# A two-layer hybrid encoder on one core: the butterflies and products of its Hyena branch on one elementwise engine instead of two

## The chip, the core and the metric

The kernel runs on one core of a Trainium2 chip. A core has a matrix engine (TensorE, PE in the profile), an elementwise engine (VectorE, DVE), an engine for functions of one operand (ScalarE, ACT), a third elementwise engine (GpSimd, POOL), and a queue from which most DMAs are issued (SyncE, SP). TensorE writes its results to PSUM; all other working data lie in SBUF. Each engine works through its own queue of instructions in order and waits on semaphores for the others.

The metric is the device time of one execution in microseconds (us), the median of several runs.

## The reference

The reference is an encoder trunk of two layers on 512 tokens of width 1024, all in float32:

```python
for i in range(DEPTH):                                   # DEPTH = 2
    hn = rmsnorm(h, ln_mix[i])
    (aq, ak, av, hy, gq, gk, gv, go, glr, gates) = split_cols(hn @ w_in[i], IN_SPLITS)
    y_a = attention_mixer(aq, ak, av, ...) @ w_br_attn[i]
    spec = hyena_filter_spectra(z_pos, window, hy_w1[i], ...)        # long filters, as spectra
    y_b = hyena_mixer(hy, hy_conv[i], spec, hy_skip[i]) @ w_br_hyena[i]
    y_c = gla_mixer(gq, gk, gv, go, glr, ...) @ w_br_gla[i]
    gate = jax.nn.sigmoid(gates.reshape(B, L, N_BRANCH, D_MODEL))
    mixed = gate[:, :, 0] * y_a + gate[:, :, 1] * y_b + gate[:, :, 2] * y_c
    h = h + mixed @ w_out[i]
    h = h + memory_cross_attention(rmsnorm(h, ln_x[i]), rmsnorm(mem, ln_mem[i]), ...)
    h = h + jnp.square(jax.nn.relu(rmsnorm(h, ln_mlp[i]) @ mlp_w1[i])) @ mlp_w2[i]

def long_conv(u, spec, skip):                            # u is (1, 512, 512 channels)
    y = jnp.fft.irfft(jnp.fft.rfft(uf, n=2 * L, axis=1) * spec, n=2 * L, axis=1)[:, :L]
    return (y + uf * skip).astype(u.dtype)

def hyena_mixer(u, conv_w, spec, skip):
    u = short_conv(u, conv_w)                            # width 3, on v, x1 and x2
    v, x1, x2 = jnp.split(u, 3, axis=-1)
    z = x1 * long_conv(v, spec[:, 0], skip[0])
    return x2 * long_conv(z, spec[:, 1], skip[1])
```

What matters here is the Hyena branch: for each layer two long convolutions in a row, each a forward transform, a product with a filter's spectrum, and an inverse transform.

## The kernel before

All large products are done by three matmuls in a 32-bit format that TensorE rounds (`mm3`, L249): an operand is split into a rounded high half and the rest, and high x high, high x low and low x high are added in PSUM (L251, L252, L253). The high half is made by ScalarE (L235), the low one by VectorE as a subtraction (L236). Weights arrive in chunks of 128x1024 (`wr`), and every chunk is split in the same way into `wh` and `wl`, with three buffers each. So every product, and the split of every weight chunk, has a step on VectorE.

**The Fourier transforms are matmuls.** A transform of 1024 points is taken apart into four small ones of 128x128 cosine and sine matrices (`dft`) and butterflies between their results. A spectral product (`spectral`, L798) is done for 256 channels and one of the two convolutions of a layer. There are thus four for a layer: `hyena_half` runs for c = 0 and 1, and each half runs the two convolutions one after the other (o = 0 and 1), since the second works on the result of the first. One spectral product does the following:

- it loads four tiles F of the filter's spectrum (128x512 each) from device memory;
- forward matmuls into PSUM, four tiles; ScalarE copies two of them to SBUF (`held`), VectorE adds and subtracts the other two to and from these (L611, `ts`);
- the butterfly `quarters` (L614): four results from the sums; two by one wide instruction each (128x512, L618 and L619), two by two narrow ones each (128x256, L622);
- the complex products with F, for each of the four results g: two wide multiplications (L823, L824) and two narrow additions (L825, L826);
- the inverse butterflies: L830 to L834, then four wide L838, each followed by a split of its result into `pqh` (ScalarE) and `pql` (VectorE);
- inverse matmuls with `dft` into PSUM.

After the first convolution the result is multiplied by x1 into `z` (L870), which is split for the next one. After the second it is copied by ScalarE to `yt`, transposed by TensorE, and scaled and multiplied by x2 on VectorE into `yb` (L887).

**The filters** (`filters`, L637) are computed for each layer, for both convolutions and both halves: a small network on position features, a window, matmuls with `dft`, and at the end the same `quarters` (L749) into four tiles `ff`, which go to device memory as F (L751). Layer 0's run ahead of the attention, between about 100 and 290 us. Layer 1's run as pieces within layer 0's MLP.

**Which engine does what** is told for these parts by a table of letters, V for VectorE and P for GpSimd (L170). `engs` (L221) turns a row of it into engines. `fq` and `hq` are the four results of `quarters` in the filters and in a spectral product; `hp` the four complex products; `hi` the inverse butterflies, the first four letters L830 to L834, the last four the four L838:

```python
ENGS = dict(fq='PPVV', hq='VVPV', hp='VVPV', hi='VVVVPVPV', lx='VVVVVVVV', aw='V',
            mx='VPVPVPVP')
```

GpSimd also has other work that the table doesn't tell: the adds of the merge (L1117, three branches into `acc`), sums of the filters (L673, L674, L711).

**What sets the order.** The branches are generators; ORDER0 and ORDER (L145 to L156) list the order in which their steps are written out (`hy0`, `hy1` are the two halves of Hyena, `me` the merges, `ga` the gates). On that a scheduler puts each engine's queue in order, by what is ready when by its own cost model, with priorities: splits of weights are put ahead by 200 (SPLIT_AHEAD), late steps back by the numbers of LATE (L167), as the inverse matmuls (`hc`, 100). While Hyena's steps run, TensorE also has the projections of gates and branches to do (`xh`, `xl` with `wh`, `wl`; `yah`, `ych`), which need only weights.

Of the kernel before, what the change touches and what calls it, by code (L numbers as in the profile page):

```python
# [93 lines left out]
def laid_out(a):  # L94
# [43 lines left out]
    for s_ in range(2):  # L138
# [28 lines left out]
LATE = dict(ff=50, fn=100, fr=100, fs=50, gA=100, gm=35, go=150, gq=35, gs=150, gt=10, hc=100, ht=150,  # L167
            kt=300, pt=100, pv=150, qt=200, xs=200, xt=35, xv=10)

ENGS = dict(fq='PPVV', hq='VVPV', hp='VVPV', hi='VVVVPVPV', lx='VVVVVVVV', aw='V',  # L170
            mx='VPVPVPVP')
SMALL = 768

# [1 line left out]
class Trunk:  # L175
# [45 lines left out]
    def engs(self, key):  # L221

        return [self.nc.vector if x == "V" else self.nc.gpsimd for x in ENGS[key]]

# [1233 lines left out]
```

## Time and profile before

| | |
|---|---|
| median of 3 runs | 2281.23 us (2280.59 to 2283.82) |
| profiled execution, its own time | 2285.21 us |
| its span | 2283.4 us |
| mean granted TensorE clock | 0.985 of full speed |
| TensorE busy | 2197.6 us, 96%, 11032 matmuls |
| VectorE busy | 1533.5 us, 67%, 2455 instructions |
| ScalarE busy | 1001.0 us, 44%, 1623 instructions |
| GpSimd busy | 422.6 us, 19%, 353 instructions |
| DMA | 233.56 MB, mean 102 GB/s |

Busy times are shares of the span. In the rows of this document L236 is line 236 of the kernel; a row of a group gives the line, the engine, the operation, the tile written, the tiles read, their shape (partitions x elements) and type, the count, the busy time in us, the mean duration of one in ns, and the idle time of the engine just before them with the engine, tile and line that ended most of it.

Hyena's products run from about 410 to 600 us (layer 0) and from about 1530 to 1720 us (layer 1). VectorE's busy share is highest in the first 300 us (0.9 and more in some slices), where layer 0's filters and attention lie.

### The profile page before, as it was taken

To read this page: it belongs to the slowest core of one execution; us is meant where nothing else is said; L and a number is where in the kernel's file an instruction comes from. 1 tells how busy PE (TensorE), PEld (TensorE's weight loads), DVE (VectorE), ACT (ScalarE), POOL (GpSimd) and SP (SyncE) were. 2 spreads that over 40 slices of the span, in tenths; PEclk is the share of its full clock that TensorE was granted. 3 is DMA by queue.
4 is the path that set the end of the run, shared out by engine and by line. 5 is a ranking of instruction groups with operands and counts; after the bars stand their busy time and mean duration, and the time that the engine had idled before them with its cause. 6 is when DMAs were issued, how large, how long until landed. Compare 5 with 4: busy or idle time off the path is not lost.

```text
span 2283.4 us, 28957 instructions
## 1 busy us (share of the span) xinstructions
PE 2197.6 (96%) x11032; PEld 1831.6 (80%) x11032; DVE 1533.5 (67%) x2455; ACT 1001.0 (44%) x1623; POOL 422.6 (19%) x353
## 2 busy tenths in 40 slices
PE   7989999998899999999999989999989999999999
PEld 5877888786678878888887878887867888888887
DVE  7798855979665765766485685667886566344445
ACT  6666844332344544443335576343323444433231
POOL 1142101224220101111060230102252101000004
PEclk9999999999999999999999999999989999999999
DMA  6442123223143243433344211332232322333332
GB/s 236 136 139 83 56 84 116 65 83 106 59 148 112 63 127 102 134 120 100 100 155 146 94 51 56 91 117 74 77 109 91 130 75 74 102 99 95 98 94 95
DMA packets 80098, 233.56 MB, mean 102 GB/s; under 512 B 9174, under 2 KB 11222, under 8 KB 79960
## 3 DMA queue, kind: packets, MB, share of 16 engines
q1 hardware_dynamic: 76792, 225.95, 31.2%
q0 software_dynamic: 3168, 5.77, 0.9%
q8 instruction: 86, 1.41, 0.3%
q14 instruction: 52, 0.43, 0.1%
HBM read 214.91 MB, written 16.78 MB: 101 GB/s over the span
## 4 chain that ended last, share of the span: by engine, by line
PE 78%; DVE 14%; issue 3%; ACT 2%; DMA 2%; POOL 1%; SPq 0%; DVEq 0%; POOLq 0%; ACTq 0%
PE ps L251 24%; PE ps L253 24%; PE ps L252 24%; DVE wl L236 3%; PE ps L557 1%; DVE ts L823 1%; ACT wh L235 1%; PE ps L566 1%; DMA F<-F 1%; PE ps L568 1%; DVE u L824 1%; PE ps L544 1%; DVE ts L611 1%; PE ps L545 0%; DMA wr<-in_w_in_dram 0%
## 5 line engine op out<-in xcount | busy, mean ns | idle before, releaser
L236 DVE TENSOR_TENSOR wl<-wr,wh 128x1024 fp32r<-128x1024 f32 x324 | 415.1, 1284 | 244.0 <-ACT wh L235 239.7
L235 ACT CAST wh<-wr 128x1024 fp32r<-128x1024 f32 (+1 forms) x328 | 341.0, 1042 | 507.1 <-PE ps L252 424.2
L253 PE MATMUL ps<-xh,wl 128*128 128x512 f32 x1344 | 530.6, 395 | 17.5 <-DVE wl L236 17.5
L251 PE MATMUL ps<-xh,wh 128*128 128x512 f32 x1344 | 532.9, 397 | 4.2 <-ACT wh L235 3.9
L252 PE MATMUL ps<-xl,wh 128*128 128x512 f32 x1344 | 531.1, 395 | 0.0
L253 PEld LDWEIGHTS ps<-xh,wl 128*128 128x128 f32 x1344 | 254.6, 189 | 73.8 <-DVE wl L236 22.5
L251 PEld LDWEIGHTS ps<-xh,wh 128*128 128x128 f32 x1344 | 254.8, 190 | 58.2 <-ACT wh L235 5.5
L252 PEld LDWEIGHTS ps<-xl,wh 128*128 128x128 f32 x1344 | 254.9, 190 | 50.0
L253 PE MATMUL ps<-hdh,wl 128*128 128x512 f32 x512 | 199.4, 390 | 0.0
L252 PE MATMUL ps<-hdl,wh 128*128 128x512 f32 x512 | 199.4, 390 | 0.0
L251 PE MATMUL ps<-hdh,wh 128*128 128x512 f32 x512 | 199.2, 389 | 0.0
L1374 DVE TENSOR_TENSOR macc<-ps,macc 128x512 f32<-128x512 f32 x96 | 65.9, 690 | 89.1 <-PE ps L253 88.9
L252 PEld LDWEIGHTS ps<-hdl,wh 128*128 128x128 f32 x512 | 96.1, 188 | 19.9
L253 PEld LDWEIGHTS ps<-hdh,wl 128*128 128x128 f32 x512 | 96.1, 188 | 19.8
L251 PEld LDWEIGHTS ps<-hdh,wh 128*128 128x128 f32 x512 | 96.1, 188 | 19.7
L1376 POOL TENSOR_TENSOR macc<-macc,rb 128x512 f32<-128x512 f32 x16 | 23.5, 1469 | 398.4 <-DVE macc L1374 398.4
L251 PE MATMUL ps<-wh,xh 128*128 128x256 f32 x320 | 91.7, 286 | 0.0
L252 PE MATMUL ps<-wl,xh 128*128 128x256 f32 x320 | 91.5, 286 | 0.0
L253 PE MATMUL ps<-wh,xl 128*128 128x256 f32 x320 | 91.1, 285 | 0.0
L1358 DVE TENSOR_TENSOR rl<-rl 128x512 f32<-128x512 f32 x64 | 44.6, 697 | 64.8 <-ACT rl L1357 64.8
L352 POOL TENSOR_TENSOR hsum<-hsum,hsq 128x512 f32<-128x512 f32 x30 | 43.6, 1454 | 168.3 <-ACT hsq L350 168.3
L1357 ACT ACTIVATE rl<-ps 128x512 f32<-128x512 f32 x64 | 37.9, 592 | 77.9 <-PE ps L253 77.9
(405 smaller groups left out, 4522.1 us busy)
## 6 DMA issues: line engine op xcount, KB each, us to landing
wr<-in_mlp_w_dram SPq DMA_DIRECT2D x128, 512.0 KB, 3.6
wr<-in_w_in_dram SPq DMA_DIRECT2D x108, 512.0 KB, 3.7
wraw<-in_x_wv_dram SPq DMA_DIRECT2D x16, 512.0 KB, 5.5
wr<-in_x_wk_dram SPq DMA_DIRECT2D x16, 512.0 KB, 3.7
F<-ff SPq DMA_DIRECT2D x32, 256.0 KB, 3.2
F<-F SPq DMA_DIRECT2D x32, 256.0 KB, 4.9
wr<-in_w_out_dram SPq DMA_DIRECT2D x16, 512.0 KB, 3.6
wr<-in_x_wq_dram SPq DMA_DIRECT2D x16, 512.0 KB, 3.7
```

Of the source, the lines that this page charges most:

```text
L235: r = self.nc.scalar.copy(hi, src)
L236: (lo_eng or self.nc.vector).tensor_tensor(lo, src, hi, op=ALU.subtract)
L251: mm(out, lh, rh, start=start, stop=False, skip_group_check=True)
L252: mm(out, lh, rl, start=False, stop=False, skip_group_check=True)
L253: mm(out, ll, rh, start=False, stop=stop, skip_group_check=True)
L352: eng.tensor_tensor(self.hsum, self.hsum, sq, op=ALU.add)
L544: nc.tensor.matmul(s, QH[:, tk], K2, start=True, stop=False)
L557: nc.tensor.transpose(pt[:, k, i * P:(i + 1) * P], Pn[i][:, (2 * kp + k) * P:(2 * kp + k + 1) * P], self.ident)
L1357: nc.scalar.activation(r, ps, AF.Relu)
L1358: nc.vector.tensor_tensor(r, r, r, op=ALU.mult)
L1374: nc.vector.tensor_tensor(acc[m], ps, acc[m], op=ALU.add)
L1376: nc.gpsimd.tensor_tensor(acc[m], acc[m], rb, op=ALU.mult)
```

## The change

Four entries of the table of engines are rewritten, so that no letter P is left in them:

```diff
-ENGS = dict(fq='PPVV', hq='VVPV', hp='VVPV', hi='VVVVPVPV', lx='VVVVVVVV', aw='V',
+ENGS = dict(fq='VVVV', hq='VVVV', hp='VVVV', hi='VVVVVVVV', lx='VVVVVVVV', aw='V',
             mx='VPVPVPVP')
```

With it these instructions go from GpSimd's queue to VectorE's: in each of the eight spectral products the two narrow halves of one result of L622, one each of L823, L824, L825 and L826, and two of the four L838; in each of the eight filters L618 and L619. `mx` and the adds that are written with `nc.gpsimd` stay as they are. The operations, tiles and buffers are the same; the scheduler orders all queues anew.

In VectorE's queue in layer 0's filters this is the difference (a - stands before the change, a + after it). `ts` are the sums of L611, `held` what ScalarE copied, `ff` the filter's results, `wl` the low half of a weight chunk, made of `wr` and `wh`:

```order
 L611 TENSOR_TENSOR ts_868<-ps_825,held_852 128x512
-L236 TENSOR_TENSOR wl_75<-wr_69,wh_71 128x1024
+L618 TENSOR_TENSOR ff_870<-ts_866,ts_802 128x512
+L619 TENSOR_TENSOR ff_871<-ts_866,ts_802 128x512
 L622 TENSOR_TENSOR ff_872<-ts_868,ts_806 128x256 x2
 L622 TENSOR_TENSOR ff_873<-ts_868,ts_806 128x256 x2
+L236 TENSOR_TENSOR wl_75<-wr_69,wh_71 128x1024
```

L618 and L619 are in VectorE's queue now, and the weight's low half comes after the four `ff` instead of ahead of them.

In layer 0's first spectral product VectorE's queue read like this before, from the last multiplications to the first `pql`. `u` and `held` are the four results that are multiplied by F, L781 and L783 the short convolution of another step, L1113 a merge:

```order
L825 TENSOR_TENSOR u_4351<-u_4351 128x256
L831 TENSOR_TENSOR ts_4346<-held_4324,u_4350 128x512
L781 SCALAR_TENSOR_TENSOR u_4269<-ps_4244,consts,u_4269 128x511
L826 TENSOR_TENSOR u_4351<-ts_4348 128x256
L783 SCALAR_TENSOR_TENSOR u_4269<-ps_4244,consts,u_4269 128x511
L832 TENSOR_TENSOR ts_4328<-held_4344,u_4351 128x512
L833 TENSOR_TENSOR ts_4348<-held_4344,u_4351 128x256
L834 TENSOR_TENSOR ts_4348<-u_4351,held_4344 128x256
L236 TENSOR_TENSOR wl_75<-wr_70,wh_71 128x1024
L236 TENSOR_TENSOR pql_4551<-held_4324,pqh_4550 128x512
```

After the change the same place reads:

```order
L825 TENSOR_TENSOR held_4344<-held_4344 128x256
L781 SCALAR_TENSOR_TENSOR u_4269<-ps_4244,consts,u_4269 128x511
L826 TENSOR_TENSOR held_4344<-ts_4328 128x256
L783 SCALAR_TENSOR_TENSOR u_4269<-ps_4244,consts,u_4269 128x511
L825 TENSOR_TENSOR u_4351<-u_4351 128x256
L1113 SCALAR_TENSOR_TENSOR acc_4390<-gt_1720,ps_4377 128x512
L826 TENSOR_TENSOR u_4351<-ts_4348 128x256
L236 TENSOR_TENSOR wl_75<-wr_70,wh_71 128x1024
L830 TENSOR_TENSOR ts_4326<-held_4324,u_4350 128x512
L831 TENSOR_TENSOR ts_4346<-held_4324,u_4350 128x512
```

`held_4344`, the result that GpSimd had, is now treated on VectorE; the split `wl_75` stands behind the products and ahead of L830 to L834; before, it stood behind these.

In layer 0's last spectral product, VectorE's queue from its third inverse butterfly on was before:

```order
L834 TENSOR_TENSOR ts_5438<-u_5441,held_5434 128x256
L838 TENSOR_TENSOR u_5440<-ts_5416,ts_5418 128x512
L236 TENSOR_TENSOR pql_5525<-held_5414,pqh_5524 128x512
L838 TENSOR_TENSOR u_5441<-ts_5436,ts_5438 128x512
L236 TENSOR_TENSOR pql_5530<-u_5440,pqh_5529 128x512
```

And it is now:

```order
L834 TENSOR_TENSOR ts_5438<-u_5441,held_5434 128x256
L838 TENSOR_TENSOR held_5414<-ts_5416,ts_5418 128x512
L887 SCALAR_TENSOR_TENSOR yb_5499<-ps_5494,consts,u_4269 128x2x128 x2
L887 SCALAR_TENSOR_TENSOR yb_5511<-ps_5506,consts,u_4298 128x2x128 x2
L236 TENSOR_TENSOR ybl_5503<-yb_5499,ybh_5502 128x512
L236 TENSOR_TENSOR pql_5525<-held_5414,pqh_5524 128x512
L236 TENSOR_TENSOR ybl_5515<-yb_5511,ybh_5514 128x512
L838 TENSOR_TENSOR u_5440<-ts_5416,ts_5418 128x512
L838 TENSOR_TENSOR held_5434<-ts_5436,ts_5438 128x512
L838 TENSOR_TENSOR u_5441<-ts_5436,ts_5438 128x512
L236 TENSOR_TENSOR pql_5530<-u_5440,pqh_5529 128x512
```

The four L838 are all in this queue, and `yb` of the other half's result (L887, which reads a transposed tile of PSUM) and its split have moved from behind the last `pql` to between the first L838 and the first `pql`. In the same product two `wl` of the gates' weights stand among the first L824 to L826, where two of them stood between L830 and L832.

## Rows read from the trace of the kernel before

**Rows 1.** The page: busy time of each engine, and the chain of waits by engine.

```profile
PE 2197.6 (96%) x11032; PEld 1831.6 (80%) x11032; DVE 1533.5 (67%) x2455; ACT 1001.0 (44%) x1623; POOL 422.6 (19%) x353
...
PE 78%; DVE 14%; issue 3%; ACT 2%; DMA 2%; POOL 1%; SPq 0%; DVEq 0%; POOLq 0%; ACTq 0%
```

**Rows 2.** Windows: PE, PEld, DVE, ACT, POOL busy us (instructions), clock, DMA, GB/s.

```profile
410.00:600.00 190.00, 173.91 (x857) 144.66 (x855) 158.50 (x228) 58.20 (x86) 57.45 (x38) 0.96 0.25 78
1530.00:1720.00 190.00, 175.86 (x868) 146.56 (x867) 156.87 (x236) 58.60 (x84) 59.78 (x38) 0.96 0.27 84
100.00:290.00 190.00, 173.60 (x1068) 149.55 (x1067) 171.48 (x320) 131.06 (x253) 55.61 (x61) 0.97 0.29 93
820.00:1080.00 260.00, 258.54 (x1210) 214.65 (x1210) 171.28 (x257) 111.27 (x163) 33.46 (x31) 1.00 0.37 116
```

**Rows 3.** Timeline, PE: start, us, line, operands, [idle before <-releaser].

```profile
433.68 0.50 PE L253 MATMUL ps<-xh,wl 128*128 128x512 f32 x1 [2.71 <-DVE wl L236]
...
539.82 0.80 PE L251 MATMUL ps<-zh,dft 128*128 128x256 f32 x2 [4.43 <-ACT zh L235]
...
580.40 0.80 PE L253 MATMUL ps<-yah,wl 128*128 128x512 f32 x1 [3.94 <-DVE wl L236]
...
1673.30 0.79 PE L253 MATMUL ps<-ych,wl 128*128 128x512 f32 x1 [4.57 <-DVE wl L236]
```

**Rows 4.** Timeline, DVE: one butterfly stretch, one row of the third, one of the filters.

```profile
118.56 3.60 DVE L622 TENSOR_TENSOR ff<-ts,ts 128x256 f32<-128x256 f32 x4
...
416.16 0.68 DVE L618 TENSOR_TENSOR held<-ts,ts 128x512 f32<-128x512 f32 x1
...
419.72 1.77 DVE L823 TENSOR_TENSOR ts<-u,F 128x512 f32<-128x512 f32 x1
...
425.81 0.41 DVE L826 TENSOR_TENSOR u<-ts 128x256 f32<-128x256 f32 x1
426.15 0.68 DVE L823 TENSOR_TENSOR ts<-u,F 128x512 f32<-128x512 f32 x1
426.75 0.67 DVE L1113 SCALAR_TENSOR_TENSOR acc<-gt,ps 128x512 f32<-128x512 f32 x1
...
432.41 1.21 DVE L236 TENSOR_TENSOR wl<-wr,wh 128x1024 fp32r<-128x1024 f32 x1
435.44 1.12 DVE L236 TENSOR_TENSOR pql<-held,pqh 128x512 fp32r<-128x512 f32 x1 [1.82 <-ACT pqh L235]
...
536.72 1.74 DVE L824 TENSOR_TENSOR u<-u,F 128x512 f32<-128x512 f32 x1
```

**Rows 5.** Groups on POOL, 410 to 600 us: count, busy, mean ns, idle.

```profile
L838 POOL TENSOR_TENSOR held<-ts,ts 128x512 f32<-128x512 f32 x8 | 13.6, 1705 | 24.3 <-DVE ts L832 14.3 <-issue 7.6 <-DVE ts L834 2.3
...
L1117 POOL TENSOR_TENSOR acc<-acc,gt 128x512 f32<-128x512 f32 x6 | 10.2, 1702 | 14.0 <-DVE gt L1116 13.9
```

**Rows 6.** The same groups view, on DVE.

```profile
L236 DVE TENSOR_TENSOR wl<-wr,wh 128x1024 fp32r<-128x1024 f32 x22 | 29.8, 1367 | 12.2 <-ACT wh L235 12.1
...
L823 DVE TENSOR_TENSOR ts<-u,F 128x512 f32<-128x512 f32 x8 | 9.3, 1157 | 0.0
...
L824 DVE TENSOR_TENSOR u<-u,F 128x512 f32<-128x512 f32 x8 | 8.7, 1085 | 0.0
...
L236 DVE TENSOR_TENSOR pql<-held,pqh 128x512 fp32r<-128x512 f32 x8 | 7.4, 925 | 3.6 <-ACT pqh L235 3.6
...
L838 DVE TENSOR_TENSOR u<-ts,ts 128x512 f32<-128x512 f32 x8 | 6.5, 816 | 0.0
...
L622 DVE TENSOR_TENSOR u<-ts,ts 128x256 f32<-128x256 f32 x8 | 5.2, 686 | 0.0
...
L824 DVE TENSOR_TENSOR held<-held,F 128x512 f32<-128x512 f32 x4 | 4.9, 1230 | 0.0
...
L619 DVE TENSOR_TENSOR u<-ts,ts 128x512 f32<-128x512 f32 x4 | 4.4, 1090 | 0.0
...
L1116 DVE SCALAR_TENSOR_TENSOR gt<-gt,ps 128x512 f32<-128x512 f32 x6 | 4.1, 676 | 0.8 <-PE ps L253 0.8
```


## The prediction

> **What bounds the kernel now.** The page first: TensorE is busy for 96% of the span and carries 78% of the chain of waits, VectorE is busy for 67% and carries 14%, GpSimd 19% and 1% [rows 1]. So a change to VectorE's and GpSimd's work can only be worth what TensorE loses by waiting for them. The windows say where that is [rows 2]. In the two stretches in which the four spectral products of a layer run (410 to 600 us, 1530 to 1720 us) TensorE is idle for 190 - 173.9 = 16.1 and 190 - 175.9 = 14.1 us, while VectorE is busy for 158.5 and 156.9 of 190. In the stretch of layer 0's filters (100 to 290) TensorE is idle for 16.4 and VectorE busy for 171.5 of 190. In the stretch where layer 1's filters run inside layer 0's MLP (820 to 1080) TensorE is idle for 1.5 of 260. The rest of the 86 us that TensorE stands still lies elsewhere and is not touched.
>
> Next TensorE's timeline, for what ends those waits [rows 3]. Three waits of layer 0's spectral stretch are the ones over 2 us, 2.71, 4.43 and 3.94 us: two for the low half of a weight tile (`wl`, L236 on VectorE), one for the z of L870, which VectorE makes and ScalarE rounds. None is for GpSimd. Layer 1 repeats the three; its middle one is the fourth row (4.57). So TensorE waits for VectorE's queue, in which the weight splits stand between spectral instructions.
>
> Then VectorE's timeline [rows 4]. A 128x512 instruction takes 0.68 us and the next begins 0.60 later (426.15, 426.75); a 128x256 one takes 0.41 and gives way after 0.34 (425.81, 426.15). But the same line L823 takes 1.77 at 419.72, L824 1.74 at 536.72, and four 128x256 instructions of L622 take 3.60 at 118.56 where 4 x 0.34 = 1.36 would do. Beside these GpSimd was at work on its share of the same arithmetic. The groups show that this is general [rows 6]: L824 has a mean of 1.23 and 1.09 us, L823 of 1.16. L1116, with one operand in PSUM, stays at its 0.68 though GpSimd's adds (L1117) run among it. So GpSimd's work is not free: it stretches VectorE's own.
>
> **The change part by part.** It moves 8 instructions per spectral product from GpSimd to VectorE's queue (two halves of L622, then L823, L824, L825, L826 and two of L838: four wide, 128x512, and four narrow, 128x256) and two per filter (L618, L619). Nothing else is added or taken away, but the scheduler puts VectorE's and TensorE's instructions in another order around them.
>
> *Added.* A stretch of four products gets 16 wide x 0.60 + 16 narrow x 0.34 = 15.0 us on VectorE. The upper bound for a wide one is the 1.77 us of a slowed one, where L1117 still runs.
>
> *Taken away.* From [rows 6], with 0.68, 0.41 and 1.21 us as undisturbed durations [rows 4]: `wl` 22 x 0.16 = 3.5, L823 8 x 0.48 = 3.8, L824 8 x 0.41 + 4 x 0.55 = 5.4, `pql` 8 x 0.25 = 2.0, L838 8 x 0.14 = 1.1, L622 8 x 0.28 = 2.2, L619 4 x 0.41 = 1.6; sum 19.6 us. GpSimd's adds of L1117 stay; they are 10.2 of its 57.5 us in this stretch [rows 2, 5], 18%. So 19.6 x 0.82 = 16.1 us go. VectorE's work is then 15.0 - 16.1 = -1.1 us per stretch: as good as unchanged, with one engine instead of two.
>
> *Hand-offs.* ScalarE's rounding of the first inverse tile (`pqh`) waits for GpSimd's L838, which takes 1.71 us on average [rows 5], against 0.68 on VectorE; VectorE idles for 3.6 us in the stretch for `pqh` in turn (one such wait is the 1.82 at 435.44) [rows 4, 6]. Two waits shorter by 1.0 us each: -2.0. VectorE alone thus ends a stretch 3 us earlier, 6 us for both layers. That is the small end.
>
> The Trainium skill (SBUF — State Buffer, "Who interferes with whom") has it that a VectorE instruction with two SBUF inputs and a GpSimd instruction that reads SBUF shut each other out, the second one waiting for all of the first. By that each stretch would shed nearly all of GpSimd's moved time, 57.5 - 10.2 = 47.3 us, and VectorE's work would fall by 32 us instead of 1.1. The rows give less: a wide instruction that is caught grows by 1.1 us (0.68 to 1.77), and many of the moved ones run where VectorE reads PSUM or is idle; the row's figure is used.
>
> *At TensorE's waits.* The first: from L618 at 416.16 VectorE reached `wl` at 432.41, 16.25 us later [rows 4]. In the new order 13 wide and 12 narrow instructions stand between the two (L830 to L834 now come behind `wl`), 13 x 0.60 + 12 x 0.34 = 11.9 us, so `wl` ends at 416.16 + 11.9 + 1.21 = 429.3. TensorE came to its wait at 433.68 - 2.71 = 430.97. This wait goes: -2.7, or -1.7 if one of the conv instructions now put before `wl` has to wait for its matmul. The second (4.43): z stands behind L823, L824, L825 and L826 of a product, which were slowed by L823 and L824 on GpSimd and by L1117; the first two go, L1117 stays. Half: -2.2. The third (3.94): the two `wl` now stand before most of the product rather than in its second half, so TensorE gets its weights earlier; but the product ends no sooner, and TensorE comes to its inverse transform earlier and waits there. Half: -2.0. In layer 0's last product the new order also puts four L887, which wait for TensorE's transposes of the third product's result, between the first L838 and `pql`; three L838 and four `pql` are queued behind them, and TensorE's inverse transform waits for those. Its gate matmuls, which stand between, cover that; if they don't, this wait stays whole (3.94). Together -6.9 for a layer, -13.8 for both.
>
> *Clock.* The granted clock of these stretches is 0.96 on average [rows 2]: 8% of 190 us, 15 us, at the lower of the two levels (1.2 instead of 2.4 GHz), after the long waits. At most 7.6 us of work per stretch are lost to it; a third of the waits gone takes an estimated 1.2 us of that, -2.4 for both.
>
> *Filters.* Layer 1's lie where TensorE hardly waits, so they cost nothing; if that cover went, 4 x 2 x 0.60 = 4.8 us. Layer 0's four add 4.8 us to a VectorE that is 90% busy; the one that I looked at closely (118.56) gives back 3.60 - 1.36 = 2.2. The new order also puts a `wl` ahead of L498 and one behind L618 and L619. I cannot price it from rows: between -5 and +5, taken as 0.
>
> Sum: -13.8 - 2.4 + 0 = -16 us. The profiled execution took 2285.2 us (span 2283.4), 4.0 above the median of the runs, 2281.2; I take the difference off the median: **2265 us**.
>
> **Rivals.**
> 1. *VectorE is full and gets 15 us more.* If the stretching is not GpSimd's doing, or L1117 alone does it, the 15.0 us per stretch come on top: 158.5 + 15 = 173.5 busy of 190, and every split stands further behind. With two thirds of 2 x 15.0 on the path: +20, 2301 us. It decides where less than 13 us (15.0 - 2.0) per stretch are given back. Against it: L1116 keeps its 0.68 while L824 takes 1.74. The Trainium skill (Perfetto Trace Analysis, "Optimizing Scalar/DVE Operations") says that with VectorE saturated, giving work to GpSimd may make sense, which speaks for this rival, and in the next sentence that between these two it might not help. The trace agrees with the second sentence.
> 2. *Exchange.* The waits are shifted, not shortened: splits come earlier, `pq` later, and the reordering in layer 0's filters eats the rest. -3 us, 2278. For it: VectorE's work hardly changes (-1.1 us).
> 3. *All of it.* The three waits of each layer go, and with them the lower clock: 2 x (2.71 + 4.43 + 3.94) + 2 x 6 = 34 us, 2247. For it: the small groups that I left out can only add to what is given back; against it: L1117 stays, and the filters' tiles F still have to come from memory.
>
> **How the numbers follow.** Forecast 62% (2255 to 2276); exchange 14%; all of it 15%; slower 9%. Below 2249 I leave 7%, above 2282 10%: range 2249 to 2282. 0.2% is 4.6 us, about what can be told here. Faster than 2276.6: the forecast, all of it and a little of exchange, 0.79; slower than 2285.8: 0.08; the same 0.13.
>
> **What would show it.** Right: VectorE's busy time about as before (1533 us, within 15) though it has 72 rows more; L823 and L824 with means near 0.68; POOL near 300 us; TensorE's waits over 2 us in each spectral stretch down from three to one or two; `pqh` no longer waiting for GpSimd. Wrong: L823 and L824 still well over 1 us with GpSimd quiet; VectorE's busy time up by 30; or the idle time of TensorE unchanged with its waits moved to `pql`; or a new wait of several us between 100 and 290.

## The result and the profile after

The changed kernel takes 2248.59 us (median of 4 runs, 2246.91 to 2250.57) against 2282.53 of the kernel before in the same measurement: the ratio is 0.9851, 95% interval 0.9834 to 0.9868. It is 34 us faster. The forecast was 16 us faster, 2265, in a range from 2249 to 2282. So the direction was right, and the forecast size was half of what came. The two profiled executions differ by 37.5 us of span (2283.4 to 2245.9), a little more than the medians, since the one of before lay 2.7 us above its median and the one of after (2247.7) 0.9 below.

The page of the changed kernel, busy times and the chain of waits by engine:

```profile
PE 2184.4 (97%) x11032; PEld 1824.0 (81%) x11032; DVE 1517.5 (68%) x2535; ACT 1002.9 (45%) x1623; POOL 308.8 (14%) x273
...
PE 81%; DVE 9%; ACT 3%; issue 3%; DMA 2%; POOL 1%; SPq 0%; POOLq 0%; DVEq 0%; ACTq 0%
```

Against [rows 1], VectorE runs 80 instructions more and is busy 16 us less; its share of the chain falls from 14% to 9%. TensorE does the same 11032 matmuls in 13.2 us less, and stands still for 61.5 us instead of 85.8.

Where that lies is read by windows cut at the same places of the program: from the last matmul of the attention in a layer to its first L1156 (the output projection). First the two stretches in the kernel before (columns as in [rows 2]):

```profile
394.50:643.70 249.20, 230.28 (x1131) 189.36 (x1130) 192.09 (x279) 79.09 (x114) 73.47 (x50) 0.97 0.27 83
1521.90:1769.80 247.90, 229.93 (x1129) 189.17 (x1128) 193.68 (x280) 79.27 (x114) 78.36 (x50) 0.97 0.27 86
```

and after:

```profile
392.60:625.80 233.20, 225.84 (x1131) 187.36 (x1130) 186.41 (x311) 79.85 (x114) 29.70 (x18) 0.99 0.28 89
...
1502.70:1733.50 230.80, 222.92 (x1129) 184.28 (x1128) 188.43 (x312) 79.53 (x114) 30.06 (x18) 1.00 0.29 92
```

The stretches are 16.0 and 17.1 us shorter, 33.1 of the 37.5. TensorE's idle time in them falls from 18.9 to 7.4 and from 18.0 to 7.9 us; the rest, 4.4 and 7.0 us, is the same number of matmuls done at a granted clock of 0.99 and 1.00 instead of 0.97. VectorE has 32 instructions more in each and is busy 5.7 and 5.3 us less. Outside, the part ahead of the first stretch is 1.9 us shorter (394.5 to 392.6), the MLP of layer 0 with layer 1's filters is as long as before (540.3 and 540.5), layer 1's attention is 1.5 and the end 1.2 us shorter.

TensorE's waits. [rows 3] has three of layer 0 and one of layer 1; the other two long ones of layer 1 before the change are these:

```profile
1560.98 0.50 PE L253 MATMUL ps<-xh,wl 128*128 128x512 f32 x1 [2.66 <-DVE wl L236]
...
1706.77 0.80 PE L253 MATMUL ps<-yah,wl 128*128 128x512 f32 x1 [3.88 <-DVE wl L236]
```

After the change, those that answer to them and the largest others:

```profile
527.91 0.51 PE L251 MATMUL ps<-zh,dft 128*128 128x256 f32 x2 [1.90 <-ACT zh L235]
...
545.10 0.49 PE L253 MATMUL ps<-ych,wl 128*128 128x512 f32 x1 [1.15 <-DVE wl L236]
...
562.59 0.51 PE L253 MATMUL ps<-yah,wl 128*128 128x512 f32 x1 [0.36 <-DVE wl L236]
...
600.74 0.57 PE L253 MATMUL ps<-ybh,wl 128*128 128x512 f32 x1 [1.61 <-DVE wl L236]
...
1643.35 0.51 PE L253 MATMUL ps<-ych,wl 128*128 128x512 f32 x1 [1.32 <-DVE wl L236]
...
1671.82 0.50 PE L253 MATMUL ps<-yah,wl 128*128 128x512 f32 x1 [1.17 <-DVE wl L236]
...
1732.00 0.49 PE L251 MATMUL ps<-mixh,wh 128*128 128x512 f32 x1 [2.22 <-ACT mixh L235]
```

The first wait (2.71) is gone, the one for z fell from 4.43 to 1.90, the one at the `yah` matmuls from 3.94 to 0.36. In layer 1 the first is gone too, the wait for a weight split at `ych` (fourth row of [rows 3]) fell from 4.57 to 1.32, the one at `yah` from 3.88 to 1.17. So the three long waits fell by 8.8 us in layer 0 and by 8.6 in layer 1; the rest of TensorE's idle time that went, 2.7 and 1.5 us, is the balance of smaller waits. In layer 0 two of 1.58 and 1.43 us are gone, while one at the weights of `ybh` grew from 0.52 to 1.61. Of the waits of over 2 us in the two stretches one is left, 2.22 us for `mixh` at the very end of layer 1's, which the kernel before has as well (2.20).

The groups on VectorE between 410 and 600 us, which answer to [rows 6]:

```profile
L236 DVE TENSOR_TENSOR wl<-wr,wh 128x1024 fp32r<-128x1024 f32 x25 | 33.4, 1338 | 12.1 <-ACT wh L235 12.0
L1116 DVE SCALAR_TENSOR_TENSOR gt<-gt,ps 128x512 f32<-128x512 f32 x10 | 6.6, 681 | 2.8 <-PE ps L253 2.6
L823 DVE TENSOR_TENSOR ts<-u,F 128x512 f32<-128x512 f32 x8 | 6.6, 821 | 0.0
...
L838 DVE TENSOR_TENSOR u<-ts,ts 128x512 f32<-128x512 f32 x8 | 5.5, 686 | 0.0
L236 DVE TENSOR_TENSOR pql<-held,pqh 128x512 fp32r<-128x512 f32 x8 | 5.5, 685 | 0.0
...
L824 DVE TENSOR_TENSOR held<-held,F 128x512 f32<-128x512 f32 x8 | 5.5, 683 | 0.0
L824 DVE TENSOR_TENSOR u<-u,F 128x512 f32<-128x512 f32 x8 | 5.5, 683 | 0.0
L622 DVE TENSOR_TENSOR u<-ts,ts 128x256 f32<-128x256 f32 x8 | 3.1, 417 | 0.0
...
L619 DVE TENSOR_TENSOR u<-ts,ts 128x512 f32<-128x512 f32 x4 | 2.7, 684 | 0.0
```

L824 went from 1085 and 1230 ns to 683, `pql` from 925 to 685 and no longer idles for `pqh` (3.6 us before), L622 from 686 to 417. L823 and `wl` keep a little: L1117 still runs on GpSimd beside them.

### The profile page after: what moved, and what is told of

Its sections match the earlier page's. It is cut to its first block, busy times and chain, and to the rows that moved or that the text cites. A ratio compares the mean times of both kernels' runs of the same rounds, so it can differ in the third digit from the quotient of the medians.

```text
span 2245.9 us, 28944 instructions
## 1 busy us (share of the span) xinstructions
PE 2184.4 (97%) x11032; PEld 1824.0 (81%) x11032; DVE 1517.5 (68%) x2535; ACT 1002.9 (45%) x1623; POOL 308.8 (14%) x273
## 3 DMA queue, kind: packets, MB, share of 16 engines
q8 instruction: 86, 1.41, 0.3%
## 4 chain that ended last, share of the span: by engine, by line
PE 81%; DVE 9%; ACT 3%; issue 3%; DMA 2%; POOL 1%; SPq 0%; POOLq 0%; DVEq 0%; ACTq 0%
PE ps L251 25%; PE ps L253 25%; PE ps L252 25%; DVE wl L236 2%; PE ps L557 1%; ACT wh L235 1%; DMA wr<-in_w_in_dram 1%; PE ps L544 1%; PE ps L566 1%; PE ps L568 1%; PE ps L545 0%; DVE ts L823 0%; PE ps L1312 0%; ACT p L549 0%; DMA F<-F 0%
## 5 line engine op out<-in xcount | busy, mean ns | idle before, releaser
L236 DVE TENSOR_TENSOR wl<-wr,wh 128x1024 fp32r<-128x1024 f32 x324 | 412.1, 1273 | 238.8 <-ACT wh L235 234.5
L1117 POOL TENSOR_TENSOR acc<-acc,gt 128x512 f32<-128x512 f32 x32 | 55.1, 1733 | 390.4 <-DVE gt L1116 375.0
```

The source lines that it names most:

```text
L236: (lo_eng or self.nc.vector).tensor_tensor(lo, src, hi, op=ALU.subtract)
L1117: nc.gpsimd.tensor_tensor(self.acc[m], self.acc[m], t, op=ALU.add)
```

## The experiments

Three theories were set against each other. *Contention*: GpSimd's running instructions stretch VectorE's, and that is the gain. *Late results*: what GpSimd computed came late to those who waited for it. *Order*: the new order of VectorE's queue, with the weight splits earlier, made the gain.

**GpSimd busy with work that nobody needs.** The changed kernel gets a helper, called once the sums of a product are there (six instructions) and once at its first `pqh` (two):

```diff
+    def idle_work(self, after, kind):
...
+        e.tensor_tensor(s[:, 0:4], k, k, op=ALU.add)            # k: 4 columns of the tile that starts it
...
+        for r in ((n, n, w, w, n, n) if kind == 2 else (w, w)):
+            e.tensor_tensor(s[:, r], x[:, r], y[:, r], op=ALU.add)
```

Lines are left out at the dots. There e is GpSimd, s a scratch tile, x and y are constants, n and w the first 256 and 512 columns. Its control has all of them at 4 columns. The kernel with the full ones and its control have the same queues on VectorE, TensorE, ScalarE and SyncE, instruction for instruction.

> The changed kernel, with GpSimd given back the same number and shapes of elementwise instructions in each spectral product (4 of 128x256, 4 of 128x512, two 128x4 ahead of them as a trigger), but on constants and into a scratch tile that nobody reads; they are extra work and leave the output as it is. Theory 1 (GpSimd's running instructions stretch VectorE's two-operand SBUF instructions): VectorE's wl, L823, L824, pql grow again by some 15 to 21 us per stretch of four products, TensorE's waits come back, and the time goes up by 15 to 45 us over the same kernel with 128x4 dummies, to 2265 to 2295 us. Theory 2 (what GpSimd computed came late, and VectorE and ScalarE waited for it) and theory 3 (the new order of VectorE's queue, above all the earlier weight splits, made the gain): nobody waits for the dummies and the order of VectorE, TensorE and ScalarE is that of the 128x4 kernel, so within 3 us of it.

> The same kernel as the full dummies with every dummy only 128x4: the queues of VectorE, TensorE, ScalarE and SyncE are the same instruction for instruction, GpSimd is nearly quiet. The control: by theories 1 and 2 within 5 us of the changed kernel's 2248.6; by theory 3 (order) it may differ by more, since a few places of the order differ from the changed kernel's.

Measured: 2288.1 us with the full ones (ratio to before 1.0018, 1.0009 to 1.0027), 2252.66 with the small ones (0.9863, 0.9850 to 0.9877). The idle work costs 35.4 us: all that the change had gained. The windows of the two stretches, full:

```profile
390.20:642.50 252.30, 232.49 (x1129) 191.32 (x1128) 207.07 (x312) 79.51 (x114) 77.27 (x58) 0.95 0.27 84
...
1520.60:1771.20 250.60, 229.51 (x1129) 188.21 (x1128) 210.34 (x311) 79.49 (x114) 76.86 (x58) 0.97 0.27 85
```

and small:

```profile
393.20:627.60 234.40, 225.45 (x1129) 186.61 (x1128) 187.47 (x312) 80.13 (x114) 49.62 (x58) 0.99 0.29 90
...
1503.90:1738.00 234.10, 224.52 (x1129) 185.20 (x1128) 187.85 (x312) 80.17 (x114) 47.62 (x58) 0.99 0.29 91
```

The same instructions of VectorE take 19.6 and 22.5 us longer, and the stretches are 17.9 and 16.5 us longer. Where it falls is seen in the groups on VectorE (410 to 600 us; the lines are moved by the helper: L237 is L236 of the kernel before, L623 is L622). Full:

```profile
L237 DVE TENSOR_TENSOR wl<-wr,wh 128x1024 fp32r<-128x1024 f32 x24 | 33.3, 1386 | 11.2 <-ACT wh L236 11.1
...
L237 DVE TENSOR_TENSOR pql<-held,pqh 128x512 fp32r<-128x512 f32 x8 | 7.8, 971 | 0.0
...
L623 DVE TENSOR_TENSOR held<-ts,ts 128x256 f32<-128x256 f32 x8 | 6.9, 889 | 0.0
...
L237 DVE TENSOR_TENSOR zl<-z,zh 128x512 fp32r<-128x512 f32 x4 | 4.4, 1092 | 0.0
L1130 DVE SCALAR_TENSOR_TENSOR gt<-gt,ps 128x512 f32<-128x512 f32 x6 | 4.1, 681 | 4.7 <-PE ps L254 4.7
```

Small:

```profile
L237 DVE TENSOR_TENSOR wl<-wr,wh 128x1024 fp32r<-128x1024 f32 x25 | 32.4, 1297 | 14.8 <-ACT wh L236 14.7
...
L237 DVE TENSOR_TENSOR pql<-held,pqh 128x512 fp32r<-128x512 f32 x8 | 5.6, 697 | 0.0
...
L623 DVE TENSOR_TENSOR held<-ts,ts 128x256 f32<-128x256 f32 x8 | 3.1, 416 | 0.0
...
L237 DVE TENSOR_TENSOR zl<-z,zh 128x512 fp32r<-128x512 f32 x4 | 2.7, 685 | 0.0
```

`pql`, `zl` and the butterflies, the steps right ahead of TensorE, are stretched by 0.27 to 0.47 us each; L1130 (L1116 before), with one operand in PSUM, stays at 681. TensorE's waits with the full ones in layer 0:

```profile
427.86 0.50 PE L254 MATMUL ps<-xh,wl 128*128 128x512 f32 x1 [0.33 <-DVE wl L237]
...
511.44 0.58 PE L252 MATMUL ps<-zh,dft 128*128 128x256 f32 x1 [3.85 <-ACT gt L1111]
...
572.03 0.79 PE L254 MATMUL ps<-yah,wl 128*128 128x512 f32 x1 [4.92 <-DVE wl L237]
```

In the control none of these three waits reaches 0.3 us, with the same queues: they are the contention's doing. The one at `yah` is back, 4.92 where it was 3.94. The one of 3.85 us is not the old wait for z. It stands ahead of the last six of 24 matmuls of the first z, and ScalarE's `gt` ended it. VectorE and ScalarE just before:

```profile
505.78 2.31 DVE L237 TENSOR_TENSOR wl<-wr,wh 128x1024 fp32r<-128x1024 f32 x1
```

```profile
509.33 0.62 ACT L236 CAST pqh<-held 128x512 fp32r<-128x512 f32 x1 [4.00 <-DVE held L850]
```

The `wl` of 2.31 us and the `pql` of 1.41 ahead of it (1.22 and 0.68 in the control) make L850 (L838 before) late, ScalarE waits 4.00 us for it, and `gt` stands behind that in ScalarE's queue. Layer 1 has the same wait, 3.83 us. Where the second z is due, both kernels wait the same 1.2 us in layer 0.

The first wait is not back: 0.33 instead of 2.71. GpSimd is busy there only up to 419.5 us, and VectorE needs 14.7 us from L618 to that `wl`, against 16.25 before and 11.96 in the changed kernel. The new order, in which the split stands ahead of L830 to L834, keeps that wait small. So order has a share at one wait of each layer, and contention carries the rest.

GpSimd's idle work could also have cost time by holding up GpSimd's own adds (L1117), for which ScalarE's `mixh` waits. It did not: TensorE waits for `mixh` 0.5 and 2.2 us in the two stretches with the full ones and 0.4 and 2.2 with the small ones.

**The parts of the change by themselves.** Single entries of the table, the others as before: only hq, hp and hi; only fq; only hi; only hq and hp.

```diff
e3:  fq='PPVV', hq='VVVV', hp='VVVV', hi='VVVVVVVV'
e4:  fq='VVVV', hq='VVPV', hp='VVPV', hi='VVVVPVPV'
e5:  fq='PPVV', hq='VVPV', hp='VVPV', hi='VVVVVVVV'
e6:  fq='PPVV', hq='VVVV', hp='VVVV', hi='VVVVPVPV'
```

> Only the spectral products' part is moved (hq, hp, hi), the filters' L618 and L619 stay on GpSimd. By the stages of the two traces (-16.0 and -17.1 us in the two stretches with the products, -1.9 ahead of them): 2250 to 2253 us. If the filters' part is worth more than that (their L622 and L619 were stretched from 0.34 and 0.68 to 0.78 and 1.09): up to 2260.

> Only the filters' L618 and L619 are moved (fq), the spectral products stay as before. By the stages: -1.9 us at layer 0's filters and 0 in the MLP, 2279 to 2282 us. As the prediction had it: between -5 and +5 us, taken as 0.

> Only the inverse butterflies are moved (hi: two L838 for each product), filters and the rest of the products stay as before. Contention by the books of the trace of before: VectorE gets 8 x 0.60 = 4.8 us per stretch and gets back 3.5 to 4.2 (what L838 on GpSimd stretched), so its work is unchanged: -2 to +3 us, 2281 to 2286. Late results (GpSimd's L838 takes 1.71 us against 0.68, and ScalarE's pqh and VectorE's pql wait for it, last in the chain before TensorE's inverse transform): -8 to -16 us, 2267 to 2275.

> Only the butterfly and the complex product of the third result are moved (hq, hp), L838 and the filters stay. Contention by the books: per stretch 10.2 us added, 16 to 17 given back, and GpSimd's chain of 8 us per product is gone: most of the spectral gain, 2256 to 2266. Late results of L838 as the main cause: at most a third of the gain, 2272 to 2280.

| moved | us | before | ratio, 95% interval |
|---|---|---|---|
| hq, hp, hi | 2254.17 | 2282.88 | 0.9872 (0.9856 to 0.9887) |
| fq | 2278.96 | 2282.88 | 0.9986 (0.9977 to 0.9995) |
| hi | 2279.13 | 2282.66 | 0.9983 (0.9974 to 0.9992) |
| hq, hp | 2260.82 | 2282.66 | 0.9905 (0.9891 to 0.9918) |

The spectral part is worth 28.7 us, the filters' 3.9, hq and hp 21.8, hi 3.5. The parts add up to 29.2 of 34.0. The spectral part lies 1 us above its first range, fq at the edge of its own, and hq with hp within what contention by the books gave ("by the books" is the sum of what VectorE gets and what it gets back). hi lies just below the range that contention by the books gave (-2 to +3) and far from the -8 to -16 of late results. hi takes away L838's contention together with its late results, so the late results by themselves are not measured; with the contention they are worth 3.5 us.

**The same added work on VectorE.** The helper with e = VectorE, and its control with 4 columns:

```diff
-        nc, e = self.nc, self.nc.gpsimd
+        nc, e = self.nc, self.nc.vector
```

> The changed kernel, with the eight idle instructions for each product (4 of 128x256, 4 of 128x512, constants into a scratch tile) on VectorE instead of GpSimd: 15 us more work for VectorE in each stretch of four products, GpSimd quiet. It measures what a us of VectorE's time costs there. If VectorE's queue is the path in these stretches nearly one for one (as the 20 us per stretch of the idle GpSimd work cost 17 to 18): 2 x 13 = 26 us over the control with 128x4, 2275 to 2285. If added work finds gaps and only stretched instructions at the wrong places hurt: 5 to 10 us, 2258 to 2266.

> The control of the last: the idle instructions on VectorE only 128x4. Both ways: within 6 us of the changed kernel's 2248.6, by ten small instructions per product and some shifts in the order.

Measured: 2263.53 and 2253.01 us, 10.5 apart; the first lies within the lower of its two ranges. The windows with the full ones:

```profile
390.40:626.40 236.00, 223.37 (x1129) 184.85 (x1128) 203.72 (x351) 79.68 (x114) 29.26 (x18) 1.00 0.28 90
1504.30:1746.40 242.10, 227.61 (x1129) 187.93 (x1128) 206.97 (x352) 79.77 (x114) 32.80 (x18) 0.97 0.28 88
```

and with the small ones:

```profile
391.60:626.10 234.50, 225.23 (x1129) 186.70 (x1128) 190.81 (x352) 80.38 (x114) 27.73 (x18) 0.99 0.29 91
1505.00:1738.50 233.50, 223.84 (x1129) 184.58 (x1128) 192.51 (x352) 79.86 (x114) 31.70 (x18) 1.00 0.29 91
```

VectorE is busy for 12.9 and 14.5 us more, 27.4, for 10.5 us of time: 0.38 us per us. The idle work on GpSimd made VectorE busy for 42.1 us more and cost 35.4: 0.84 per us. Neither is one price. By stretches, the time that a us of VectorE cost was 0.91 and 0.73 for stretching (17.9 for 19.6, 16.5 for 22.5) and 0.12 and 0.59 for added work (1.5 for 12.9, 8.6 for 14.5). Added work was cheaper in both, by a factor that differs widely. The likely reason is that the scheduler knows of added instructions and puts them where the queue has room, while stretching falls on whatever runs, `pql` and `zl` among it; no run here tests that. The order of VectorE's queue also differs between these last two kernels in many places, so 0.38 is less sure than 0.84.

**The two engines side by side, by themselves.**

> A kernel by itself that leaves out the whole computation: on tiles of the same shapes it runs VectorE alone, GpSimd alone, and both side by side, by VectorE's operands (two in SBUF at 128x256, 128x512 and 128x1024, one in PSUM, one operand only), and last GpSimd with 128x4. Contention as in the traces: two SBUF operands go from 0.60 per instruction to 0.60 plus a large part of GpSimd's own time; one operand in PSUM stays at its value. If the two engines exclude each other fully, the time of the pair is the sum of both alone; if they share, it is shorter than the sum. GpSimd's 128x4 should stretch little.

This kernel was executed once. VectorE's timeline; the L32 rows are instructions into different tiles, L46 is VectorE alone, L54 with GpSimd's 128x512 (9 instructions), L72 the same with one operand in PSUM, L84 beside GpSimd's 128x4:

```profile
8.13 0.69 DVE L32 TENSOR_TENSOR h<-a,b 128x512 f32<-128x512 f32 x1
8.74 0.69 DVE L32 TENSOR_TENSOR k<-a,b 128x512 f32<-128x512 f32 x1
...
10.01 17.40 DVE L46 TENSOR_TENSOR d<-a,b 128x512 f32<-128x512 f32 x24
...
40.52 25.88 DVE L54 TENSOR_TENSOR d<-a,b 128x512 f32<-128x512 f32 x24
...
133.84 17.37 DVE L72 TENSOR_TENSOR d<-ps,b 128x512 f32<-128x512 f32 x24
...
171.30 17.41 DVE L84 TENSOR_TENSOR d<-a,b 128x512 f32<-128x512 f32 x24
```

GpSimd's groups in it: L56 beside L54, L74 beside L72, L50 alone:

```profile
L56 POOL TENSOR_TENSOR g<-h,k 128x512 f32<-128x512 f32 x9 | 14.4, 1603 | 0.7
...
L74 POOL TENSOR_TENSOR g<-h,k 128x512 f32<-128x512 f32 x9 | 11.4, 1265 | 0.7
L50 POOL TENSOR_TENSOR g<-h,k 128x512 f32<-128x512 f32 x9 | 11.4, 1262 | 0.7
```

With two operands in SBUF, VectorE loses 8.5 us to nine GpSimd instructions that take 11.4 alone, and these take 14.4. With an operand in PSUM neither loses anything; GpSimd's 128x4 cost nothing that is seen. The Trainium skill (SBUF — State Buffer, "Who interferes with whom") has both cases right by kind. On the size, its single rule calls the port pair that VectorE and GpSimd share "an exclusive lock". Taken for whole instructions, that would make an estimated 17.4 + 11.4 = 28.8 us here, and the pair takes 25.88: the loss is three quarters of GpSimd's own time. That does not refute the rule. In this loop each VectorE instruction writes the tile of the one before, and they follow each other 0.73 us apart (17.40 / 24) instead of the 0.61 of the L32 rows and the 0.60 of the kernel. With 24 x 0.60 + 11.4 the sum would be 25.8, just what the pair takes. So the run gives the price of the contention, 0.94 us for each GpSimd 128x512, and does not tell full exclusion of a shorter part of each instruction from a partial one.

The pairs with 128x256 (19.48 us), with 128x1024 (47.12 us, 18 GpSimd instructions) and with one operand only (19.49 us) have no run of VectorE alone to compare with and are not read here.

**Further adds on VectorE.** e7 is the changed kernel with L1117 on VectorE; e8 has L352 (default engine) and L965 there too; e12 all elementwise work of GpSimd that is left.

```diff
-                    nc.gpsimd.tensor_tensor(self.acc[m], self.acc[m], t, op=ALU.add)
+                    nc.vector.tensor_tensor(self.acc[m], self.acc[m], t, op=ALU.add)
```

> The changed kernel with the merge's adds (L1117, 32 instructions) on VectorE as well. Contention by the books: 16 x 0.60 = 9.6 us added per layer against 5.8 and 7.8 that L1117 still stretches, so VectorE gets 2 to 4 us more per layer while TensorE waits in few places: -3 to +3 us, 2246 to 2252. If any overlap with GpSimd costs a TensorE wait one for one: -6 to -10 us.

> The same with the adds of squares for the norms (L352) and the subtraction L965 on VectorE too. By the books L352 stretches VectorE by 9 us per cross attention and L965 by 2.8 per layer, and 30 x 0.60 + 8 x 0.60 are added; TensorE hardly waits in the cross attention, so most of it is covered: -4 to +4 us against e7. L965 waits in the front of the attention, where TensorE does wait: at best -3.

> All elementwise work that GpSimd still has in e8 goes to VectorE too (L408, L452, L673, L674, L711, L1010, L1266, L1376, L1377, the split at L1008): some 50 us of VectorE work more, some 20 us of stretching gone. Contention with TensorE waiting in the first 390 us: 2205 to 2222. If VectorE, at 0.8 busy in the front, is the bound there: 2225 to 2240, worse than e8's 2223.8.

Measured: 2237.4 (ratio to before 0.9804, 0.9790 to 0.9817), 2223.81 (0.9748, 0.9733 to 0.9763) and 2241.62 us (0.9823, 0.9809 to 0.9838). The expectations for e7 and e8 counted VectorE's work by the books and came out too small: 11 and 14 us were gained, more than either range of each had. e12 lies just above its second range. By the two prices above e7 would gain 4 (13.6 us of stretching gone, 19.2 added). Part of the rest is late results: in the changed kernel ScalarE's `mixh` waits 15.0 and 15.6 us for GpSimd's L1117 in the two stretches, and TensorE waits 2.22 us for `mixh` at the end of layer 1's; in e7 that wait is gone. Of e8's further 14 us (between the profiles), 8.3 lie ahead of the end of layer 0's attention (391.2 to 382.9) and 7.5 in layer 1's attention (336.4 to 328.9), while layer 0's MLP is 2.6 longer. e8 is the fastest kernel of the study. e12 is 18 us slower than it: a wait of 3.71 us for `xp` stands in each cross attention that e8 does not have, here layer 0's,

```profile
738.47 1.91 PE L1312 MATMUL ps<-consts,xp 128*128 128x128 f32 x7 [3.71 <-DVE xp L1308]
```

and the part up to the end of layer 0's attention takes 389 us instead of 383. Which of e12's ten lines costs how much was not tried, and why is open. Around the new wait VectorE is not full (busy for 25.9 us of the 38 from 700 to 738). So some of GpSimd's work is better left where it is; the runs do not say by what to know it.

## Why the prediction was half right

*What bounds it, and that GpSimd's work is not free* held: the first experiment and the pair show it directly. "VectorE is full and gets 15 us more" was to decide where less than 13 us per stretch are given back; 20.7 and 20.3 were (5.7 and 5.3 less busy, with 15.0 added). "All of it" (2247 us, given 15%) is what came in size: its 22.2 us of waits stand against 21.7 of idle time, its 12 us of clock against 11.4. But the waits that it named fell by 17.4, and smaller ones made up the rest, so its closeness is in part luck.

*Added*, 15.0 us per stretch: the rows after bear the durations out (683 and 417 ns, as undisturbed ones before); it is 80 rows in all (8 x 8 and 8 x 2), not the 72 of the signs. *Taken away*, 16.1: between 410 and 600 us the eight groups gave 15.4 (by the means before and after), so the size of these was right. The some 5 us above it come from groups that were left out as small: L834, L825, L826, L618 and L830 give 5.2 in layer 0's stretch. So the balance of VectorE's work was -5.7 and -5.3 us and not -1.1. *Hand-offs* were given -4 for both layers, outside the sum; hi alone gave -3.5, with L838's contention in it.

Two terms of the sum failed, *At TensorE's waits* and *Clock*.

1. *At TensorE's waits* took -6.9 per layer, -13.8; the idle time fell by 11.6 and 10.1, 21.7. The first wait was right, and so was its working: `wl` starts 11.96 us after L618 in the changed kernel (414.30 to 426.26), where 11.9 was reckoned. The second and third were halved, and they fell by 2.5 of 4.4 and 3.6 of 3.9 in layer 0, by 3.3 of 4.6 and 2.7 of 3.9 in layer 1. For the third the reason was "the product ends no sooner", which rests on the balance of -1.1; by the balance that came, it ends sooner. Layer 1's second wait was read as a repeat of the one for z; it is one for a weight split, at `ych`. The smaller waits, 4.2 us in all, were not counted.
2. *Clock* took -1.2 per layer, of the 7.6 us that it held the low clock to cost at most. TensorE's busy time for the same matmuls fell by 4.4 and 7.0 us, 11.4 against 2.4: this is the larger miss, 9.0 us against 7.9. Before the change the granted clock is 0.52 to 0.68 in the 5 to 6 us behind each of the three long waits of a layer. Behind the one for z, in layer 0, it is this, and then full again:

```profile
540.00:545.00 5.00, 4.95 (x18) 3.99 (x19) 5.00 (x10) 0.00 (x0) 0.00 (x0) 0.52 0.00 0
545.00:550.00 5.00, 5.00 (x23) 4.02 (x22) 3.87 (x6) 1.68 (x2) 2.88 (x2) 1.00 0.27 63
```

   After the change the clock of the two stretches was 0.99 and 1.00. The mistake was to take a sixth of that loss, less than the share of the waits that the forecast itself let go (6.9 of 16.1 and of 14.1 us). A wait that is shortened, and not gone, can take its low clock with it: in layer 1 two of the three are left at 1.32 and 1.17 us, and the clock is 1.00.
3. *Filters*: 0 between -5 and +5 was taken, and fq alone gives -3.9. Layer 1's cost nothing within the MLP, as forecast.

The mean prices of the experiments do not close the sum. At 0.84 for the 41.0 us given back and 0.38 for the 30 added they make -34.4 + 11.4 = -23, with the filters -27 of the measured -34. Some 7 us are not assigned. (hi's -3.5 is not to be added: its L838 are among the 41 and the 30.)

The added wait at L887 in layer 0's last product did not show: no wait of TensorE for `pql` stands among those of the changed kernel's stretch.

## What to carry to other kernels

Before you split elementwise work between VectorE and GpSimd, compare the durations of one VectorE line with two SBUF operands where GpSimd is quiet and where it isn't: what it grows by is the price of the split, and it falls on the steps that other engines wait for. A balance of the engine's busy time is not enough: here a us of stretching cost more time than a us of added work in both stretches, by a factor that is not settled. And where a long wait of TensorE goes, count the clock with it.

## What was not expected of the hardware

GpSimd's nine 128x512 additions took 1.26 us each alone and 1.60 beside VectorE, and cost VectorE 0.94 us each; the two engines together did 17.3 us of single work in 14.4 us (11.4 of GpSimd, 14.4 - 8.5 = 5.9 of VectorE), so there is some gain from both running, but a small one. Against VectorE's pace of 0.60 us in the kernel there is none (24 x 0.60 + 11.4 = 25.8, and the pair took 25.88). VectorE alone did one 128x512 instruction in 0.73 us, so to do GpSimd's additions itself would have cost it less than to run beside them.
